# Issue order of weight splits and of the first matrix product in a one-core decoder kernel

## The chip, the cores and the metric

The kernel runs on one core of one Trainium2 chip. The metric is the device time of one execution in microseconds (us), as the median of several runs; lower is better. A core has five engines with queues of their own that are followed in order: TensorE (PE in the profile; its weight loads are PEld), VectorE (DVE), ScalarE (ACT), GpSimd (POOL) and SyncE (SP), which issues the DMA transfers here.

## The reference, cut to what matters

One step of a decoder layer, for a prompt of 2048 tokens and for 8 samples of 8 tokens that share all weights. The width is 1024, everything is float32.

```python
def _rmsnorm(x, g):
    x = x * lax.rsqrt(jnp.mean(x * x, axis=-1, keepdims=True) + 1e-5)
    return x * g

mem_k, mem_v = rmsnorm(mem, g_mem) @ w_ck, rmsnorm(mem, g_mem) @ w_cv   # 256 memory tokens
h = rmsnorm(x, g_mix)
q, k, v, u = split(h @ w_in)                     # 8 query heads, 2 kv heads, 512 pool channels
attn = window_attention(q, k, v, sinks)          # window 128, ALiBi
pool = pool_mixer(u) @ w_pool * pool_scale       # windows 2, 4, 8, 16
x = x + concat(attn, pool) @ w_out               # output projection
h = rmsnorm(x, g_cross)
p = softmax((h @ w_cq) @ mem_k.T / 16)           # 4 heads
x = x + (p @ mem_v) @ w_co                       # cross output
h = rmsnorm(x, g_ffn)
x = x + square(relu(h @ w_up)) @ w_down          # hidden 4096
y = rmsnorm(x, g_final)
```

The keys, values and pool histories are outputs too.

## The kernel before, in words

**Precision and splits.** Each float32 operand of a large product is split in two: a high part, rounded by a cast on ScalarE, and a low part, the difference, taken on VectorE. A product is then three matmuls per contraction step: high x high, high x low, low x high. For activations `rnd` (L94) and `Norm.apply` (L226) make the two parts. For weights the class `Stream` does it: `emit` (L125) takes the next item of one fixed list, loads its 512 KB through SP into one of six raw tiles `f` (L131), casts it into one `w` tile (L132) and subtracts into another (L133). There are twelve `w` tiles, so six weights can be split at once; a product gives a pair back when it has read it. `next` (L143) hands out a split weight and then calls `pump` (L137), which emits as long as two `w` tiles are free and fewer than five weights are ready.

**Order.** The program is written in one order, but the framework that builds the kernel decides the order of each engine's queue. It goes by readiness in a model of its own: of the instructions that are ready it takes the one that was written first, so a split that was written later can be queued ahead of an addition whose product isn't done yet. Waits between engines are put in by the framework. `tc.keep_in_program_order` (L214) holds the norm's matmul behind everything that was written before it on TensorE.

**Prologue** (L361). Fourteen warm-up matmuls of `ones` and `ident` (L366), whose result is not used; then the memory is loaded and split (L379, L380), its squares are summed (L202, L205, L206), and w_ck and w_cv are multiplied by it in sixteen chunks of 24 matmuls (`mm3`, L108: lines 111 to 113). After the third chunk the norm is finished (L404). Then w_cq and mem_k are folded into one matrix A, and mem_v and w_co into one matrix B. Both go through DRAM (`a_s`, `b_s`), stored by `put_fold` (L329).

**Superblocks** (L480). The tokens are worked in three superblocks of two blocks each, 384 and 384 tokens in the first two, 256 and 256 + 64 in the third. Each goes through:

- the input projection, attention and pooling, interleaved;
- the output projection: `dense` (L267) over eight chunks of 128 output columns for each block, 24 matmuls (L280 to L282) a chunk. Its `evac` is `add_evac` (L890): an addition to x on VectorE (L892), then `Norm.sq`, a Square on ScalarE (L205) and, for all but the first chunk, an addition to the sum of squares on GpSimd (L206). The last three chunks run for block 0 first and then for block 1;
- the norm of each block: `fin` (L209) is one matmul that sums over partitions (L214), two activations (L217, L218) and three operations on VectorE (L219 to L221); `apply` makes the normalised activations, eight steps of L232 on VectorE, L233 on ScalarE, and L235 on VectorE or GpSimd in turn. It is written one chunk after the block's last chunk, in pieces;
- the cross attention: `cross` (L912) takes the four weights of A's first half, then for each tile of 128 tokens 24 matmuls (lines 111 to 113), then A's second half. The fourth weight is read from the seventh contraction step on. In the third superblock the cross attention of the samples is interleaved (L966);
- the cross output: `dense` again, with B and `add_evac2` (L1091, addition L1093); its last four chunks run for block 0, then block 1;
- the feed-forward part, eight groups of `up` (L1138; evicted by L1130 to L1134) and `down` (L1143). The first group of `up` runs four chunks for block 0 and then four for block 1.

**Which splits stand around the ends.** When the eighth chunk of the output projection is fetched, three of its weights hold six `w` tiles, and the first three weights of A are emitted into the rest. After its last eviction is written, the next call of `next` emits three more: A's fourth weight and two of its second half. At the cross output four weights hold eight tiles, two weights of `up` are emitted ahead, and after the last eviction four more: the third and fourth chunk's of the first group and two of the second group.

Of the kernel before, what the change touches and what calls it, by code (L numbers as in the profile page):

```python
# [11 lines left out]
AF = mybir.ActivationFunctionType  # L12
ALU = mybir.AluOpType

P = 128
# [36 lines left out]
def kernel(ctx: ExitStack, tc: tile.TileContext, io, nW=12, nF=6, nT=8):  # L52
    nc = tc.nc
# [18 lines left out]
    ident = sb("ident", P)  # L72
    make_identity(nc, ident)
    ones = sb("ones", P)
# [16 lines left out]
    def f32(ap):  # L91
        return ap.bitcast(F32)
# [12 lines left out]
    def w8(t):  # L105
        return t[:].rearrange("p (k c) -> p k c", c=P)
# [8 lines left out]
    class Stream:  # L115
        def __init__(self):
            self.items = deque()
            self.ready = deque()
            self.resW = 0
            self.resF = 0  # L120

        def add(self, key, *raw, eng=None):
            self.items.append((key, raw, eng or nc.vector))

        def emit(self):  # L125
            key, raw, eng = self.items.popleft()
            th, tl = WS.get(), WS.get()
            r = FS.get()
            w = 1024 // len(raw)
            for i, src in enumerate(raw):  # L130
                nc.sync.dma_start(r[:, w * i:w * i + w], src)  # L131
            nc.scalar.copy(th[:], r[:, 0:1024])  # L132
            eng.tensor_tensor(tl[:], r[:, 0:1024], f32(th[:]), ALU.subtract)  # L133
            FS.put(r)
            self.ready.append((key, th, tl))

# [14 lines left out]
    S = Stream()  # L151
# [32 lines left out]
    class Norm:  # L184
# [4 lines left out]

        def sq(self, k, eng=None):  # L190
            n = self.n
            if self.on_pe:
                t = TS.get()
                if eng is None:
                    nc.scalar.activation(t[:, 0:n], self.x(k), AF.Square)
                else:
                    eng.tensor_tensor(t[:, 0:n], self.x(k), self.x(k), ALU.mult)
                nc.tensor.matmul(self.pm[:, 0:n], ones[:], t[:, 0:n], start=k == 0, stop=k == 7)
                TS.put(t)
            elif self.acc is None:  # L200
                self.acc = TS.get()
                nc.scalar.activation(self.acc[:, 0:n], self.x(k), AF.Square)  # L202
            else:
                t = TS.get()
                nc.scalar.activation(t[:, 0:n], self.x(k), AF.Square)  # L205
                self.add.tensor_tensor(self.acc[:, 0:n], self.acc[:, 0:n], t[:, 0:n], ALU.add)  # L206
                TS.put(t)

        def fin(self):  # L209
            n = self.n  # L210
# [56 lines left out]
    def dense(keys, blks, hi, lo, evac, head=2, tail=3, after=None, piece=8, seq=None):  # L267
        nch = len(keys)
        loaded, left, done = {}, {}, {0: 0, 1: 0}
        fetched = 0  # L270
        for c, b in seq or order(nch, head, tail):
            while fetched <= c:
                loaded[fetched] = S.next(keys[fetched])
                left[fetched] = 2
                fetched += 1
            th, tl = loaded[c]
            n = blks[b].n
            ps = MM.get()
            for k in range(8):
                nc.tensor.matmul(ps[:, 0:n], w8(th)[:, k, :], hi(b, k), start=k == 0, stop=False)  # L280
                nc.tensor.matmul(ps[:, 0:n], w8(th)[:, k, :], lo(b, k), start=False, stop=False)  # L281
                nc.tensor.matmul(ps[:, 0:n], w8(tl)[:, k, :], hi(b, k), start=False, stop=k == 7)  # L282
                if k < 7 and k % piece == piece - 1:
                    yield
            evac(c, b, ps)
            MM.put(ps)
            left[c] -= 1
            if left[c] == 0:
                WS.put(th, tl)
            flush()  # L290
            done[b] += 1
            if after is not None and done[b] == nch:
                later.append([DEF[b], lambda b=b: after(b)])
            yield
# [66 lines left out]
    def prologue():  # L361
        S.resW, S.resF = 1, 0
        mx = [XT[1][:, 0:1024], XT[1][:, 1024:2048]]
        mem = lambda k: mx[k // 4][:, 256 * (k % 4):256 * (k % 4 + 1)]
        warm = AUX.get()
        for _ in range(14):  # L366
            nc.tensor.matmul(warm[:, 0:P], ones[:], ident[:], start=True, stop=True)
        AUX.put(warm)
        nc.sync.dma_start(vec[:], io["vec"])
        nc.sync.dma_start(mx[0][:, 0:512], io["mem"][:, 0:512])  # L370
        S.emit()
        hm = Act(256)
        nm = Norm(256, mem, add=nc.vector)
        for i in range(4):
            if i:
                nc.sync.dma_start(mx[i // 2][:, 512 * (i % 2):512 * (i % 2) + 512], io["mem"][:, 512 * i:512 * (i + 1)])
            for k in range(2 * i, 2 * i + 2):
                g = vec[:, V_GMEM + k:V_GMEM + k + 1]
                nc.scalar.activation(hm.hi(k), mem(k), AF.Copy, scale=g)  # L379
                nc.vector.scalar_tensor_tensor(hm.lo(k), mem(k), g, f32(hm.hi(k)), ALU.mult, ALU.subtract)  # L380
        S.emit()
        for k in range(8):
            nm.sq(k)
        S.pump()
        def evac(a, dst, c, ps):
            t = TS.get()
            nc.vector.tensor_tensor(t[:, 0:256], ps[:, 0:256], nm.r[:, 0:256], ALU.mult)
            MM.put(ps)
            nc.sync.dma_start(dst[:, 256 * c:256 * (c + 1)], t[:, 0:256])
            rnd(t[:, 0:256], a.hi(c), a.lo(c))  # L390
            TS.put(t)

        pend, outs = [], []
        for name, dst in (("ck", io["mk"]), ("cv", io["mv"])):
            a = Act(256)
            outs.append(a)
            for c in range(8):
                th, tl = S.next((name, c))
                ps = MM.get()
                mm3(ps[:, 0:256], range(8), lambda k: w8(th)[:, k, :], lambda k: w8(tl)[:, k, :], hm.hi, hm.lo)  # L400
                WS.put(th, tl)
                pend.append((a, dst, c, ps))
                if name == "ck" and c == FINC:
                    nm.fin()  # L404
                if name == "cv" or c >= FINC:
                    while pend:
                        evac(*pend.pop(0))
                flush()
                if (name, c) == N1C:
                    norm1(blk[0][0], N1W)  # L410
        TS.put(nm.r)
        hm.free()
        mk, mv = outs
        norm1(blk[0][1], N1Q)
        for c in range(8):
            th, tl = S.next(("cq", c))
            for hf in range(2):
                ps = MM.get()
                for h2 in range(2):
                    ks = [(hf * 2 + h2) * 2, (hf * 2 + h2) * 2 + 1]  # L420
                    mm3(ps[:, 256 * h2:256 * h2 + 256], ks, lambda k: w8(th)[:, k, :], lambda k: w8(tl)[:, k, :], mk.hi, mk.lo)
                put_fold(ps[:], lambda o: [(a_s[hf, c // 2, :, 512 * (c % 2):512 * (c % 2) + 512], o[:, 0:512])])
                MM.put(ps)
            WS.put(th, tl)
            flush()
        mk.free()
        for h in range(4):
            w = [S.next(("co", 2 * h)), S.next(("co", 2 * h + 1))]
            for mb in range(2):
                for eh in range(2):  # L430
                    ps = MM.get()
                    mm3(ps[:], range(2),
                        lambda k: mv.hi(2 * h + k, mb * P, mb * P + P), lambda k: mv.lo(2 * h + k, mb * P, mb * P + P),
                        lambda k: w[k][0][:, 512 * eh:512 * eh + 512], lambda k: w[k][1][:, 512 * eh:512 * eh + 512])
                    kt = h * 2 + mb
                    put_fold(ps[:], lambda o: [(b_s[4 * eh:4 * eh + 4, :, P * kt:P * kt + P].rearrange("e p c -> p e c"),
                                                o[:, 0:512].rearrange("p (e c) -> p e c", c=P))])
                    MM.put(ps)
                flush()
            WS.put(*w[0], *w[1])  # L440
        mv.free()
# [38 lines left out]
    def superblock(s, blks, nxt):  # L480
        last = s == 2
# [3 lines left out]
        for kv in range(2):  # L485
            for hl in range(2):
                i = 2 * kv + hl
# [401 lines left out]

        def add_evac(c, b, ps):  # L890
            bl = blks[b]
            nc.vector.tensor_tensor(bl.x(c), ps[:, 0:bl.n], bl.x(c), ALU.add)  # L892
            bl.norm.sq(c)

        def mix_hi(hl):
            return lambda b, k: k4(blks[b].q[hl] if k < 4 else blks[b].d[hl], blks[b].n)[:, k % 4, :]
# [193 lines left out]

        def add_evac2(c, b, ps):  # L1091
            bl = blks[b]
            nc.vector.tensor_tensor(bl.x(c, 0, bl.np), ps[:, 0:bl.np], bl.x(c, 0, bl.np), ALU.add)  # L1093
            bl.norm.sq(c)

        def after_co(b):
            bl = blks[b]
# [240 lines left out]
```

## Time and profile before

| what | value |
|---|---|
| time, median of 3 runs | 2636.88 us (2635.72 to 2638.27) |
| profiled execution | span 2632.9 us; the median lies 4.0 us above it |
| VectorE busy | 1304.3 us (50%) |
| ScalarE busy | 982.1 us (37%) |
| GpSimd busy | 665.8 us (25%) |
| DMA | 244.76 MB, mean 93 GB/s |

The profile is one execution, taken by the hardware profiler. Busy time is the time in which an engine worked on an instruction; the ends of matmuls are modelled. A timeline row has start and duration in us, engine, line of the kernel, operation, output and inputs by their names, shape and count; the bracket at its end has the idle time of that engine before it and the event that ended it. A window row has the window, its length, and the busy time (and count) of PE, PEld, DVE, ACT and POOL, then the granted TensorE clock as a share, the busy share of the DMA engines, and GB/s. "SPq" rows are the issue of transfers.

### The profile page before, as it was taken

The page shows a single profiled execution, that of the slowest core. Times are in us where ns is not written, and L with a number is a line of the kernel's source. Part 1 is how long each engine was busy: PE and PEld are TensorE (multiplying, and loading weights), DVE is VectorE, ACT ScalarE, POOL GpSimd, SP SyncE. Part 2 cuts the span into 40 slices and gives each one's busy share as a digit, 9 for nine tenths or more (in the row PEclk, how much of TensorE's full clock was granted, in tenths as well). Part 3 has the DMA queues.
Part 4 walks back from the last instruction along what each step waited for, and adds up shares of the span by engine and source line. Part 5 has one row for each costly group of instructions (what it writes and reads, how often), then busy time and mean ns, then how long its engine had stood idle before and what let it go on. Part 6 is the DMA issues. An engine that isn't in the chain of part 4 may idle for free. (4 is left out here: it accounts for less than half of the span.)

```text
span 2632.9 us, 39258 instructions
## 1 busy us (share of the span) xinstructions
PE 2565.7 (97%) x15753; PEld 2461.6 (93%) x15753; DVE 1304.3 (50%) x2283; ACT 982.1 (37%) x1923; POOL 665.8 (25%) x723
## 2 busy tenths in 40 slices
PE   8899999999999999999999999999999999999998
PEld 8799989999999999997999999999999669999998
DVE  7567453533333367936363333334766646344334
ACT  6666342422222244824342222223354434322231
POOL 2215322311111153433241111113324214111111
PEclk9999999999999999999999999999999999999999
DMA  7843211211111123131111111112414473222210
GB/s 276 257 130 104 71 47 64 73 65 64 65 65 64 56 70 108 55 123 57 65 63 60 63 64 64 65 57 70 141 60 146 178 269 117 81 81 83 87 57 37
DMA packets 92539, 244.76 MB, mean 93 GB/s; under 512 B 16772, under 2 KB 31556, under 8 KB 91204
## 3 DMA queue, kind: packets, MB, share of 16 engines
q1 hardware_dynamic: 92356, 242.25, 27.0%
q8 instruction: 123, 2.02, 0.3%
q14 instruction: 60, 0.49, 0.1%
HBM read 219.53 MB, written 22.69 MB: 92 GB/s over the span
## 5 line engine op out<-in xcount | busy, mean ns | idle before, releaser
L280 PE MATMUL mm<-act,w 128*128 128x384 f32 (+2 forms) x2784 | 903.0, 324 | 2.6 <-ACT act L631 1.6
L281 PE MATMUL mm<-act,w 128*128 128x384 f32 (+2 forms) x2784 | 897.7, 322 | 0.7 <-DVE act L632 0.5
L282 PE MATMUL mm<-act,w 128*128 128x384 f32 (+2 forms) x2784 | 897.1, 322 | 1.2 <-DVE w L133 1.2
L132 ACT CAST w<-f 128x1024 fp32r<-128x1024 f32 x330 | 346.0, 1050 | 734.7 <-PE mm L112 459.7
L133 DVE TENSOR_TENSOR w<-f,w 128x1024 fp32r<-128x1024 f32 x330 | 425.3, 1294 | 304.7 <-ACT w L132 304.5
L111 PE MATMUL mm<-act,w 128*128 128x384 f32 (+2 forms) x1728 | 552.4, 320 | 9.3 <-ACT w L132 7.6
L113 PE MATMUL mm<-act,w 128*128 128x384 f32 (+2 forms) x1728 | 549.2, 318 | 0.5 <-DVE w L133 0.5
L112 PE MATMUL mm<-act,w 128*128 128x384 f32 (+2 forms) x1728 | 548.9, 318 | 0.0
L280 PEld LDWEIGHTS mm<-act,w 128*128 128x128 f32 x2784 | 527.6, 189 | 7.4 <-issue 2.6
L281 PEld LDWEIGHTS mm<-act,w 128*128 128x128 f32 x2784 | 527.3, 189 | 7.3 <-issue 2.6
L282 PEld LDWEIGHTS mm<-act,w 128*128 128x128 f32 x2784 | 527.2, 189 | 2.0 <-DVE w L133 1.7
L1131 POOL TENSOR_TENSOR t<-t 128x384 f32<-128x384 f32 (+2 forms) x192 | 216.2, 1126 | 1039.5 <-ACT t L1130 1039.5
L1164 DVE TENSOR_TENSOR x<-mm,x 128x384 f32<-128x384 f32 (+2 forms) x384 | 199.8, 523 | 327.9 <-PE mm L113 327.9
L111 PEld LDWEIGHTS mm<-act,w 128*128 128x128 f32 x1728 | 327.2, 189 | 11.3 <-ACT w L132 7.6
L112 PEld LDWEIGHTS mm<-act,w 128*128 128x128 f32 x1728 | 327.1, 189 | 1.0
L113 PEld LDWEIGHTS mm<-act,w 128*128 128x128 f32 x1728 | 327.0, 189 | 0.8 <-DVE w L133 0.8
L206 POOL TENSOR_TENSOR t<-t,t 128x384 f32<-128x384 f32 (+2 forms) x161 | 191.4, 1190 | 344.7 <-ACT t L205 311.7
L1134 DVE TENSOR_TENSOR act<-t,act 128x384 fp32r<-128x384 f32 (+2 forms) x192 | 102.9, 536 | 305.4 <-ACT act L1133 305.4
L1133 ACT CAST act<-t 128x384 fp32r<-128x384 f32 (+2 forms) x192 | 93.4, 487 | 235.3 <-POOL t L1131 235.3
L205 ACT ACTIVATE t<-x 128x384 f32<-128x384 f32 (+2 forms) x140 | 68.3, 498 | 153.1 <-DVE x L1093 75.6
L1130 ACT ACTIVATE t<-mm 128x384 f32<-128x384 f32 (+2 forms) x192 | 88.3, 460 | 93.2 <-PE mm L282 91.9
L111 PE MATMUL mm<-w,act 128*128 128x512 f32 x288 | 117.1, 409 | 3.0 <-ACT w L132 2.7
(187 smaller groups left out, 2211.8 us busy)
## 6 DMA issues: line engine op xcount, KB each, us to landing
f<-in_wup SPq DMA_DIRECT2D x96, 512.0 KB, 3.5
f<-in_wdn SPq DMA_DIRECT2D x96, 512.0 KB, 3.5
f<-in_win SPq DMA_DIRECT2D x30, 512.0 KB, 3.7
f<-a_s SPq DMA_DIRECT2D x24, 512.0 KB, 3.3
f<-b_s SPq DMA_DIRECT2D x24, 512.0 KB, 4.2
x<-in_x SPq DMA_DIRECT2D x6, 1536.0 KB, 7.0
f<-in_wco SPq DMA_DIRECT2D x16, 512.0 KB, 5.5
f<-in_cmk SPq DMA_DIRECT2D x16, 512.0 KB, 4.5
```

What stands on the lines that cost most here:

```text
L111: nc.tensor.matmul(ps, Wh(k), Hh(k), start=first and i == 0, stop=False)
L112: nc.tensor.matmul(ps, Wh(k), Hl(k), start=False, stop=False)
L113: nc.tensor.matmul(ps, Wl(k), Hh(k), start=False, stop=final and i == last)
L132: nc.scalar.copy(th[:], r[:, 0:1024])
L133: eng.tensor_tensor(tl[:], r[:, 0:1024], f32(th[:]), ALU.subtract)
L206: self.add.tensor_tensor(self.acc[:, 0:n], self.acc[:, 0:n], t[:, 0:n], ALU.add)
L280: nc.tensor.matmul(ps[:, 0:n], w8(th)[:, k, :], hi(b, k), start=k == 0, stop=False)
L281: nc.tensor.matmul(ps[:, 0:n], w8(th)[:, k, :], lo(b, k), start=False, stop=False)
L282: nc.tensor.matmul(ps[:, 0:n], w8(tl)[:, k, :], hi(b, k), start=False, stop=k == 7)
L1131: nc.gpsimd.tensor_tensor(q[:, 0:n], r[:, 0:n], r[:, 0:n], ALU.mult)
L1134: nc.vector.tensor_tensor(lo, q[:, 0:n], f32(hi), ALU.subtract)
L1164: nc.vector.tensor_tensor(bl.x(m), ps[:, 0:n], bl.x(m), ALU.add)
```

## The change

Three ties are added with `tc.issue_after(i)`: what the block under it writes for the engine of instruction `i` is queued behind `i` on that engine. It sets the order of that queue only, and adds no wait for `i` to finish; no operation, transfer or tile is added or removed.

- `dense` keeps what its last `evac` returned in `S.behind`. `add_evac` and `add_evac2` return their addition (VectorE) and their Square (ScalarE) for the last chunk of block 1, and nothing else does. So the weights emitted between that eviction and the next `dense`'s first eviction have their cast queued behind that Square, and their subtraction behind that addition. The loads of the raw weights are outside the block and not tied.
- The first product of the prologue (w_ck, chunk 0) is queued behind the last warm-up matmul on TensorE.

```diff
@@ class Stream
+            self.behind = []
...
-            nc.scalar.copy(th[:], r[:, 0:1024])
-            eng.tensor_tensor(tl[:], r[:, 0:1024], f32(th[:]), ALU.subtract)
+            with ExitStack() as held:
+                for i in self.behind:
+                    held.enter_context(tc.issue_after(i))
+                nc.scalar.copy(th[:], r[:, 0:1024])
+                eng.tensor_tensor(tl[:], r[:, 0:1024], f32(th[:]), ALU.subtract)
@@ Norm.sq
-                nc.scalar.activation(t[:, 0:n], self.x(k), AF.Square)
+                i = nc.scalar.activation(t[:, 0:n], self.x(k), AF.Square)
...
+            return i
@@ dense
-            evac(c, b, ps)
+            last = evac(c, b, ps)
+            S.behind = last or []
@@ prologue
-            nc.tensor.matmul(warm[:, 0:P], ones[:], ident[:], start=True, stop=True)
+            wu = nc.tensor.matmul(warm[:, 0:P], ones[:], ident[:], start=True, stop=True)
...
-                mm3(ps[:, 0:256], range(8), lambda k: w8(th)[:, k, :], lambda k: w8(tl)[:, k, :], hm.hi, hm.lo)
+                if name == "ck" and c == 0:
+                    with tc.issue_after(wu.ins):
+                        mm3(ps[:, 0:256], range(8), lambda k: w8(th)[:, k, :], lambda k: w8(tl)[:, k, :], hm.hi, hm.lo)
+                else:
+                    mm3(ps[:, 0:256], range(8), lambda k: w8(th)[:, k, :], lambda k: w8(tl)[:, k, :], hm.hi, hm.lo)
@@ add_evac (add_evac2 likewise, with the prompt's columns)
-            nc.vector.tensor_tensor(bl.x(c), ps[:, 0:bl.n], bl.x(c), ALU.add)
-            bl.norm.sq(c)
+            i = nc.vector.tensor_tensor(bl.x(c), ps[:, 0:bl.n], bl.x(c), ALU.add)
+            j = bl.norm.sq(c)
+            return [i.ins, j.ins] if (c, b) == (7, 1) else None
```

More of the change, by code (lines that the diff above doesn't have):

```diff
@@ L1092, in add_evac2 @@
             bl = blks[b]
-            nc.vector.tensor_tensor(bl.x(c, 0, bl.np), ps[:, 0:bl.np], bl.x(c, 0, bl.np), ALU.add)
-            bl.norm.sq(c)
+            i = nc.vector.tensor_tensor(bl.x(c, 0, bl.np), ps[:, 0:bl.np], bl.x(c, 0, bl.np), ALU.add)
+            j = bl.norm.sq(c)
+            return [i.ins, j.ins] if (c, b) == (7, 1) else None
         def after_co(b):
```

1 line of the change is left out of this document (added).

## The prediction

> **What bounds the kernel now.** I read the page's span and busy rows first, then TensorE's own list of waits (engine, tile and line, the releaser; total us, times, longest).
>
> ```profile
> span 2632.9 us, 39258 instructions
> PE 2565.7 (97%) x15753; PEld 2461.6 (93%) x15753; DVE 1304.3 (50%) x2283; ACT 982.1 (37%) x1923; POOL 665.8 (25%) x723
> ...
> PE aux L214 <- POOL t L206: 20.7, 9, 3.7
> ```
>
> TensorE is busy 97% of the span, so only time in which it stands still, or works at the wrong moment, can be won: 67.2 us in all. The largest single wait is the norm's one matmul (L214), which waits for the sum of squares (L206) nine times, 20.7 us together. Six of the nine stand where this change acts, once after each output projection and once after each cross output. Next I read the timelines of the start and of these places (start, duration, engine, line; in brackets the idle time before it and its releaser).
>
> ```profile
> 7.57 0.58 PE L111 MATMUL mm<-act,w 128*128 128x256 f32 x1 [7.57 <-ACT w L132]
> ...
> 9.21 0.42 PE L111 MATMUL mm<-act,w 128*128 128x256 f32 x1
> ...
> 9.43 0.41 PE L112 MATMUL mm<-act,w 128*128 128x256 f32 x1
> ...
> 9.64 5.62 PE L367 MATMUL aux<-ident,ones 128*128 128x128 f32 x28
> ...
> 15.02 0.36 PE L113 MATMUL mm<-act,w 128*128 128x256 f32 x1
> ...
> 23.02 0.28 PE L113 MATMUL mm<-act,w 128*128 128x256 f32 x1
> ...
> 8.69 2.46 DVE L380 SCALAR_TENSOR_TENSOR act<-x,vec,act 128x256 fp32r<-128x256 f32 x6
> ...
> 11.93 1.22 DVE L133 TENSOR_TENSOR w<-f,w 128x1024 fp32r<-128x1024 f32 x1
> ...
> 13.93 1.22 DVE L133 TENSOR_TENSOR w<-f,w 128x1024 fp32r<-128x1024 f32 x1
> ...
> 1.01 0.29 POOL masks.py:199 TENSOR_SCALAR_AFFINE_SELECT ident<-ident 128x128 f32<-128x128 f32 x1
> ```
>
> At the start TensorE waits 7.57 us for the first weight, does five products, and only then runs the warm-up (L367, 14 matmuls shown as 28), 5.62 us in which real work is ready. Its input, ident, was finished at 1.30.
>
> **First product behind the warm-up.** From 1.30 the 5.62 us of warm-up end at about 7.0, inside the wait that exists anyway; its cost becomes zero, and if it overran it would cost the overrun alone. What is late next? The first chunk needs the low halves of the memory activations: L380 ends at 8.69 + 2.46 = 11.15. The second chunk needs its weight's low half at 11.93 + 1.22 = 13.15, from where 22 products are left. Between 15.02 and 23.02 lie 67 products, 0.119 us each; so the second chunk ends issuing at 15.8. The third has its low half at 15.15 and ends at 15.8 + 24 x 0.119 = 18.6. Before, that was 23.02: 4.4 us gained. Against it: at 9.21 to 9.43 two products stand 0.22 apart. If the 19 products left in chunk one behind 9.43 still ran at that pace, it would end at 13.6, chunk two (a third of it slow) at about 17.2 and chunk three at 20.0: 3.0 gained. I take 4.0, nearer the first, since the warm-up then stands before the products.
>
> [...]
>
> Everything behind the third chunk (norm, evictions, stores and loads on SP) follows in order and moves with it. What could hold it back is the stage of the folds, where DMA is nearly full:
>
> ```profile
> 100.00:120.00 20.00, 17.24 (x68) 13.39 (x67) 5.24 (x5) 11.18 (x18) 1.17 (x1) 0.91 0.95 292
> ```
>
> (The last three columns are clock, DMA share and GB/s.) I keep the 4.0, since these transfers too are issued by steps that move.
>
> **Splits behind the output projection.** By the slots, three pairs of weights are split after the seventh chunk's eviction in the program: the fourth weight of A's first half, and two of its second. The cast of the first was taken early:
>
> ```profile
> 308.86 1.05 ACT L132 CAST w<-f 128x1024 fp32r<-128x1024 f32 x1 [2.81 <-PE mm L281]
> ...
> 322.52 0.55 DVE L892 TENSOR_TENSOR x<-mm,x 128x384 f32<-128x384 f32 x1
> ...
> 323.15 0.52 ACT L205 ACTIVATE t<-x 128x384 f32<-128x384 f32 x1
> ...
> 324.35 1.97 POOL L206 TENSOR_TENSOR t<-t,t 128x384 f32<-128x384 f32 x1
> ...
> 322.56 0.39 PE L111 MATMUL mm<-w,act 128*128 128x512 f32 x1
> 322.79 0.40 PE L112 MATMUL mm<-w,act 128*128 128x512 f32 x1
> ...
> 326.38 0.91 PE L214 MATMUL aux<-t,ones 128*128 128x384 f32 x2 [1.44 <-POOL t L206]
> ...
> 2060.79 0.45 PE L111 MATMUL aux<-act,act 128*64 128x512 f32 x1 [2.28 <-ACT act L233]
> ```
>
> The last addition (L892, 322.52) stays: it is queued behind the other block's norm on VectorE, not behind splits. But the first cross tile needs that fourth weight at its seventh contraction step, 322.56 (high) and 322.79 (low). Tied behind the Square, the cast runs 323.67 to 324.7 and the subtraction to 325.9, or 326.7 if it collides with L206 (0.77, worked out below); I take 326.3. So the product stalls at 322.56 to 324.7 and again to 326.3; five more products at 0.23 us end at 327.5, where L214 goes at once, its 1.44 wait gone (L206, 1.22 to 1.97 long, ends at 325.6 to 326.3). 327.5 against 326.38: **1.1 us lost**, 0.7 to 1.5 by the collision. If products of the next tile were placed into the stall, it would be a gain of up to 1.4. The second group repeats it. In the third the L214 is as late, but a wait of 2.28 us for the next norm follows (2060.79); it takes up part, and I put 0.8. Together **+3.0** (-4 to +5).
>
> **Splits behind the cross output.** Here four pairs are tied.
>
> ```profile
> 463.86 4.00 DVE L133 TENSOR_TENSOR w<-f,w 128x1024 fp32r<-128x1024 f32 x2
> 467.78 0.55 DVE L1093 TENSOR_TENSOR x<-mm,x 128x384 f32<-128x384 f32 x1
> ...
> 472.80 0.55 DVE L219 SCALAR_TENSOR_TENSOR t<-t 128x384 f32<-128x384 f32 x1
> ...
> 468.42 0.52 ACT L205 ACTIVATE t<-x 128x384 f32<-128x384 f32 x1 [3.39 <-DVE x L1093]
> ...
> 12.61 3.88 ACT L132 CAST w<-f 128x1024 fp32r<-128x1024 f32 x4
> ...
> 469.09 1.22 POOL L206 TENSOR_TENSOR t<-t,t 128x384 f32<-128x384 f32 x1 [2.31 <-ACT t L205]
> ...
> 485.48 1.02 POOL L235 TENSOR_TENSOR act<-t,act 128x384 fp32r<-128x384 f32 x1 [1.04 <-ACT act L233]
> ...
> 470.36 0.91 PE L214 MATMUL aux<-t,ones 128*128 128x384 f32 x2 [3.69 <-POOL t L206]
> ...
> 487.43 0.33 PE L281 MATMUL mm<-act,w 128*128 128x384 f32 x1
> ```
>
> The addition (L1093) does stand behind two splits: it moves from 467.78 to 463.86. The Square ended 1.16 behind it (468.42 + 0.52), so now at 465.0, and L206 2.53 behind it, so at 466.4, or 467.2 with a collision. TensorE came to L214 at 470.36 - 3.69 = 466.67, so the wait goes. But what is late next is the same norm's other end. L217's input is there, yet ScalarE first does four casts (3.88 us, to 468.9) and VectorE four subtractions: from 466.05, 4 x 1.22 gives 470.9, and 0.77 more for each that meets a POOL add (two took 4.00, not 2.46), up to 472.4. L219 then stands at 471.4 to 473.0; I take 472.4, 0.4 earlier than 472.80. The second block's first product needs the last of this norm: L235 ends at 486.50, its reader is at 487.43, so 0.93 us is all the slack. TensorE, some 3.5 us earlier, waits there. Gain: 0.4 + 0.93 = **1.3**, not 3.7 (0.7 to 2.3).
>
> [...]
>
> ```profile
> 1345.80:1349.10 3.30, 2.91 (x7) 2.31 (x8) 0.21 (x1) 1.23 (x3) 1.12 (x2) 0.50 0.70 231
> 470.40:473.80 3.40, 3.40 (x18) 3.13 (x19) 1.44 (x3) 1.41 (x3) 0.69 (x1) 1.00 0.58 186
> ...
> 1346.19 1.65 PE L214 MATMUL aux<-t,ones 128*128 128x384 f32 x2 [3.66 <-POOL t L206]
> ...
> 1349.36 0.55 DVE L219 SCALAR_TENSOR_TENSOR t<-t 128x384 f32<-128x384 f32 x1
> ...
> 1364.63 0.33 PE L281 MATMUL mm<-act,w 128*128 128x384 f32 x1
> ...
> 2203.47 1.76 DVE L133 TENSOR_TENSOR w<-f,w 128x1024 fp32r<-128x1024 f32 x1
> ...
> 2210.15 0.49 DVE L219 SCALAR_TENSOR_TENSOR t<-t 128x320 f32<-128x320 f32 x1
> ...
> 2221.02 0.90 POOL L235 TENSOR_TENSOR act<-t,act 128x320 fp32r<-128x320 f32 x1 [0.92 <-ACT act L233]
> ...
> 2221.98 0.41 PE L281 MATMUL mm<-act,w 128*128 128x320 f32 x1
> ```
>
> In the second group the same wait was followed by 3.3 us at a granted clock of 0.50 (1.65 us lost); in the first it was not. Its wait began at 1342.53, 875.86 behind the first group's, so its L219 would stand at 472.4 + 875.86 = 1348.3, 1.1 earlier; L235 ends 13.70 behind L219 as in the first group, at 1363.06, its reader is at 1364.63, a slack of 1.6: gain **2.7**. In the third there is no slack (2221.92 to 2221.98). The addition can go at 2203.47, its Square ends 1.16 later, a cast of 1.05 follows, and four subtractions end at 2210.6, or 2211.3 with a clash; behind them L219 comes 0.9 **later** than 2210.15 (0 to 1.9). Together **-3.1** (-12, when all three waits and two slow stretches are won, to +1).
>
> The moved splits issue no transfer of their own, but free the raw tiles later, so loads on SP go some 15 us later (as the cast moves from 308.86 to 323.67); what they load is six splits ahead, so I cost it at nothing, and at the length of one split, 1.22, if that lead were gone.
>
> **Sum.** -4.0 + 3.0 - 3.1 = -4.1. The profiled span of 2632.9 becomes 2628.8; the median lies 4.0 above the span (2636.88), so 2632.8. This is 0.16%; about 0.2% (5.3 us) is what a measurement of this kernel can tell from no change.
>
> **Rivals.** *Waits really go.* If the norm's steps get ahead of the casts behind the cross output, its three waits come back: 3 x 3.2 (3.69 less the half us that is left) and one slow stretch of 1.65, so -4.0 + 3.0 - 11.3 = -12.3, 2624.6; if the cross tile doesn't stall either, six waits by the mean of 20.7 / 9 = 2.3 and two slow stretches, -21, 2616. For it: L214's wait is the largest of TensorE's. Against: slack of 0 to 1.6 behind it.
> *The start's gain is lost in the folds.* DMA at 0.95 sets its own pace, and -4.0 becomes 0: -0.1, 2636.8. Against: the transfers are issued in order behind steps that move.
> *Slower: the late fourth weight.* Each stall of 3.6 us under the output projection is followed by a slow stretch: 3 x (1.1 + 1.65) = 8.3, with the start's gain down to 1 and nothing from the cross output, +7.3, 2644.2. It decides if the clock falls in all three groups and the start gives under 3. Against: it needs both.
>
> **How the numbers follow.** My forecast 0.48 (own range 2629 to 2638; a fifth of it beyond the 0.2%), waits go 0.31, folds 0.11, late weight 0.10. Faster: 0.31 + 0.10 = 0.41. Slower: most of the last, 0.09. Within: 0.50. The range leaves out the far end of the first rival and most of the slower one: 2623 to 2640.
>
> **What would show it.** Right: the warm-up before the first product, and the third chunk ended near 19; L111 of the first cross tile waiting for the cast L132 about 2 us; L214 with next to no wait; waits of 1 to 3 us for L233 or L235 in the second block's first up chunk. Wrong: L1093 still behind splits; the folds ending no earlier; L219 over 2 us earlier.

## The result, and the profile after

The changed kernel takes 2627.82 us (median of 16 runs, 2623.66 to 2634.12), the kernel before 2635.23 us on the same chip (16 runs, 2630.37 to 2639.82): a ratio of 0.9974, with a 95% interval of 0.9966 to 0.9982. The medians lie 7.4 us apart. The forecast was 2632.8 us, 4.1 us less; the time lies inside its range, but beyond the 0.2% that it had called the likeliest (the near end of the interval is 0.18%).

Lines move by a few in the new code: the cast L132 is now L136, the split's subtraction L133 is L137, Square L205 is L210, the squares' addition L206 is L211, the norm's matmul L214 is L220, L219 is L225, the apply's L233 and L235 are L239 and L241, the dense products L280 to L282 are L286 to L288, the additions L892 and L1093 are L903 and L1105, the warm-up L367 is L374.

The first rows of the profile's page and TensorE's list of waits, in the changed kernel:

```profile
span 2622.0 us, 39268 instructions
PE 2562.3 (98%) x15753; PEld 2457.1 (94%) x15753; DVE 1300.5 (50%) x2283; ACT 982.8 (37%) x1923; POOL 657.9 (25%) x723
```

```profile
PE mm L111 <- ACT w L136: 9.9, 7, 3.0
PE aux L220 <- POOL t L211: 7.9, 4, 2.7
...
PE mm L287 <- POOL act L241: 1.5, 3, 0.5
```

TensorE stands still for 59.7 us instead of 67.2. The norm's matmul waits 4 times for 7.9 us instead of 9 times for 20.7; of these four, 1.42 us is behind the third cross output, and the other three stand where the change does not act. Part of what was won is now spent on a split weight (L111 for L136: 2.40, 2.41 and 2.34 of the 9.9 us stand in the first cross tile of each superblock), and a little on the first block's apply (L287 for L241). L111 had 10.3 us before too, but there 7.6 of it was the wait for the very first weight:

```profile
PE mm L111 <- ACT w L132: 10.3, 3, 7.6
```

The timeline of the start. The warm-up runs in the idle time, the first chunk's products then follow 0.11 us behind one another (9.12, 9.23), and the next matmul behind the third chunk's last, the L220 of the memory's norm, starts at 18.89. The first row below is of the kernel before, where that matmul started at 23.14.

```profile
23.14 0.60 PE L214 MATMUL aux<-t,ones 128*128 128x256 f32 x2
```

```profile
1.35 6.06 PE L374 MATMUL aux<-ident,ones 128*128 128x128 f32 x28 [1.35 <-POOL ident masks.py:199]
7.63 0.38 PE L111 MATMUL mm<-act,w 128*128 128x256 f32 x1 [0.22 <-ACT w L136]
...
9.12 0.28 PE L111 MATMUL mm<-act,w 128*128 128x256 f32 x1
9.23 0.28 PE L112 MATMUL mm<-act,w 128*128 128x256 f32 x1
...
18.89 0.60 PE L220 MATMUL aux<-t,ones 128*128 128x256 f32 x2
```

The timeline where the first output projection ends (the column behind the two times names the engine):

```profile
317.74 0.51 PE L113 MATMUL mm<-w,act 128*128 128x512 f32 x1
320.64 0.92 PE L111 MATMUL mm<-w,act 128*128 128x512 f32 x2 [2.40 <-ACT w L136]
321.36 0.63 PE L112 MATMUL mm<-w,act 128*128 128x512 f32 x1
...
324.34 0.85 PE L220 MATMUL aux<-t,ones 128*128 128x384 f32 x2
...
318.49 0.55 DVE L903 TENSOR_TENSOR x<-mm,x 128x384 f32<-128x384 f32 x1
320.62 3.52 DVE L137 TENSOR_TENSOR w<-f,w 128x1024 fp32r<-128x1024 f32 x3 [1.58 <-ACT w L136]
...
319.79 0.99 POOL L211 TENSOR_TENSOR t<-t,t 128x384 f32<-128x384 f32 x1
```

L220 has lost its wait of 1.44, and L211 takes 0.99 instead of 1.97, since the subtractions start only when it is nearly done (320.62, where it ends at 320.78); before, two ran beside it, and took 3.95 for both where three take 3.52 here:

```profile
323.45 3.95 DVE L133 TENSOR_TENSOR w<-f,w 128x1024 fp32r<-128x1024 f32 x2
```

In exchange the seventh contraction step (L111) stands 2.40 us for the cast of A's fourth weight, and the products behind it run at 0.63 each instead of 0.40.

The timeline where the first cross output ends:

```profile
459.87 1.01 DVE L1105 TENSOR_TENSOR x<-mm,x 128x384 f32<-128x384 f32 x2
462.48 5.93 DVE L137 TENSOR_TENSOR w<-f,w 128x1024 fp32r<-128x1024 f32 x4 [1.59 <-ACT w L136]
468.33 0.55 DVE L1147 TENSOR_TENSOR act<-t,act 128x384 fp32r<-128x384 f32 x1
468.80 0.55 DVE L225 SCALAR_TENSOR_TENSOR t<-t 128x384 f32<-128x384 f32 x1
...
461.40 3.88 ACT L136 CAST w<-f 128x1024 fp32r<-128x1024 f32 x4
...
480.57 1.18 POOL L241 TENSOR_TENSOR act<-t,act 128x384 fp32r<-128x384 f32 x1 [1.04 <-ACT act L239]
...
463.39 0.86 PE L220 MATMUL aux<-t,ones 128*128 128x384 f32 x2
...
481.80 0.44 PE L287 MATMUL mm<-act,w 128*128 128x384 f32 x1 [0.53 <-POOL act L241]
```

The addition stands ahead of all four splits, and L220 starts with no wait (before: 3.69). The four splits now stand between the addition and L225, and the other end of the norm is what TensorE meets: L287 waits 0.53 for the last L241.

**Where the time went.** TensorE does the same 15,753 matmuls in both kernels. I number them in order of start and take, for the same number, the start in a run's profile less the start in the profile of before. The table has how much this difference moves over the start (to 70 us) and over each of the six places (marks, on the clock of before: 317 to 339, 1180 to 1219, 2045 to 2082 for the output projections; 462 to 492, 1338 to 1368, 2198 to 2225 for the cross outputs). Negative is earlier. The mark at 339 lies just ahead of a wait for the softmax's result (L919 in the kernel before), which gives back another 0.3 in the rows where the two weights of A's second half are held back: behind it the change stands at +1.0, and the versions with A's fourth weight free at -1.1.

| us | start | output proj. 1 | 2 | 3 | cross output 1 | 2 | 3 |
|---|---|---|---|---|---|---|---|
| forecast | -4.0 | +1.1 | +1.1 | +0.8 | -1.3 | -2.7 | +0.9 |
| the change | -3.7 | +1.3 | +0.6 | -0.1 | -2.4 | -3.7 | +0.9 |
| the change again | -3.6 | +1.2 | -0.4 | +0.2 | -2.4 | -3.7 | +0.4 |
| start's tie alone | -3.9 | 0.0 | -0.1 | +0.5 | +1.6 | +0.2 | +0.9 |
| output projection's tie alone | -0.4 | +1.2 | -0.4 | 0.0 | +1.5 | +0.2 | 0.0 |
| cross output's tie alone | -1.5 | 0.0 | 0.0 | +0.5 | -2.4 | -3.8 | 0.0 |
| start and cross output | -3.9 | 0.0 | -0.1 | +0.8 | -2.4 | -3.8 | +0.6 |
| output projection's, A's fourth weight free | +0.4 | -0.8 | -1.3 | -0.6 | +2.4 | +1.2 | 0.0 |
| cross output's on VectorE alone | -0.4 | 0.0 | -0.1 | +0.7 | -2.1 | -3.5 | +0.7 |
| two splits held back to the norm's end | -2.2 | -0.8 | -1.3 | +1.3 | -1.0 | -2.4 | +2.9 |
| the change, A's fourth weight free | -2.1 | -0.8 | -1.3 | +0.8 | -2.4 | -3.7 | -0.1 |

The change's own row sums to -7.1, next to the 7.4 of the medians. Its profile ends 11.0 earlier; about 3 of the rest are two stretches at half clock that the profile of before has, and this one has not at those places. Its windows (the third column from the end is the granted clock):

```profile
1888.50:1891.80 3.30, 3.30 (x18) 3.30 (x17) 2.44 (x5) 1.46 (x3) 0.00 (x0) 0.50 0.54 41
1929.50:1932.80 3.30, 3.30 (x15) 2.82 (x14) 1.53 (x4) 1.39 (x4) 0.00 (x0) 0.50 0.50 165
```

Such stretches, each about 3.4 us long (some twice that) and worth half of that, 1.7 (an estimate from the clock of 0.50), recur at a few places in every profile, near 1930 for one; many others lie elsewhere in each. The start differs by up to 1.5 even without its tie. So a single profile's end says little here, and each step must be read at its own place.

### The profile page after: what moved, and what is told of

It reads as the page before. It is cut to its first block, busy times and chain, and to the rows that moved or that the text cites. A ratio compares the mean times of both kernels' runs of the same rounds, so it can differ in the third digit from the quotient of the medians.

```text
span 2622.0 us, 39268 instructions
## 1 busy us (share of the span) xinstructions
PE 2562.3 (98%) x15753; PEld 2457.1 (94%) x15753; DVE 1300.5 (50%) x2283; ACT 982.8 (37%) x1923; POOL 657.9 (25%) x723
## 5 line engine op out<-in xcount | busy, mean ns | idle before, releaser
L286 PE MATMUL mm<-act,w 128*128 128x384 f32 (+2 forms) x2784 | 901.1, 324 | 2.8 <-ACT act L642 1.6
L287 PE MATMUL mm<-act,w 128*128 128x384 f32 (+2 forms) x2784 | 897.0, 322 | 3.4 <-POOL act L241 1.5
L288 PE MATMUL mm<-act,w 128*128 128x384 f32 (+2 forms) x2784 | 895.6, 322 | 1.4 <-DVE w L137 1.4
L136 ACT CAST w<-f 128x1024 fp32r<-128x1024 f32 x330 | 344.3, 1049 | 702.7 <-PE mm L112 457.6
L137 DVE TENSOR_TENSOR w<-f,w 128x1024 fp32r<-128x1024 f32 x330 | 418.4, 1276 | 305.7 <-ACT w L136 304.8
L111 PE MATMUL mm<-act,w 128*128 128x384 f32 (+2 forms) x1728 | 552.3, 320 | 2.8 <-DVE t L394 2.2
L287 PEld LDWEIGHTS mm<-act,w 128*128 128x128 f32 x2784 | 525.7, 189 | 12.7 <-POOL act L241 3.7
L286 PEld LDWEIGHTS mm<-act,w 128*128 128x128 f32 x2784 | 525.8, 189 | 7.6 <-issue 2.3
L288 PEld LDWEIGHTS mm<-act,w 128*128 128x128 f32 x2784 | 525.6, 189 | 2.2 <-DVE w L137 2.0
L1144 POOL TENSOR_TENSOR t<-t 128x384 f32<-128x384 f32 (+2 forms) x192 | 216.4, 1127 | 1038.6 <-ACT t L1143 1038.6
L1177 DVE TENSOR_TENSOR x<-mm,x 128x384 f32<-128x384 f32 (+2 forms) x384 | 199.7, 523 | 327.5 <-PE mm L113 327.5
L111 PEld LDWEIGHTS mm<-act,w 128*128 128x128 f32 x1728 | 326.8, 189 | 4.7 <-ACT t L207 2.4
L211 POOL TENSOR_TENSOR t<-t,t 128x384 f32<-128x384 f32 (+2 forms) x161 | 182.2, 1132 | 337.0 <-ACT t L210 329.6
L210 ACT ACTIVATE t<-x 128x384 f32<-128x384 f32 (+2 forms) x140 | 68.0, 498 | 161.7 <-DVE x L1105 74.5
L111 PE MATMUL mm<-w,act 128*128 128x512 f32 x288 | 116.5, 407 | 9.7 <-ACT w L136 9.7
```

Source lines behind the costliest of these rows:

```text
L111: nc.tensor.matmul(ps, Wh(k), Hh(k), start=first and i == 0, stop=False)
L1144: nc.gpsimd.tensor_tensor(q[:, 0:n], r[:, 0:n], r[:, 0:n], ALU.mult)
L1177: nc.vector.tensor_tensor(bl.x(m), ps[:, 0:n], bl.x(m), ALU.add)
```

## The experiments

My theory after the result: the start's gain is kept through the folds; the tie behind the output projection loses about 3 us and the tie behind the cross output wins more than I had put, because the norm's other end had more room than I had worked out. The rivals: that the start's gain is lost in the folds and the cross output has all of it, or that all three waits behind the cross output come back in full.

### One part at a time

The start's tie alone (both evictions return nothing to be tied behind):

```diff
-            return [i.ins, j.ins] if (c, b) == (7, 1) else None
+            return None
```

> Only the first product is tied behind the warm-up; both ties of the weight splits are left out. Theory (three parts that add up): the warm-up moves into the wait for the first weight, the third chunk ends near 18.7 us instead of 23.0, and 3.7 us are still won at 70 us and at the end of the span, apart from half-clock stretches that fall where they fall (1.7 us each). Waits of the norm's matmul under the output projection and the cross output stay as before: 1.4, 1.4, 1.0 and 3.7, 3.7, 3.1 us. Time 0.9986 of before. Rival (the folds swallow it): the gain is gone by 125 us, ratio 1.000. Rival (all of the change's gain is the start): ratio 0.997, as the whole change.

Measured: 2633.9 us, ratio 0.9991 (0.9982 to 1.0). The steps: -3.9 at 70 us, and between -2.5 and -4.7 all the way through the folds and the first superblock. The start's gain is kept; in the time it is 2.4 us, and its interval reaches from none to 4.7, so the time alone would not have settled it.

The output projection's tie alone (the first product isn't tied, and `add_evac2` returns nothing):

```diff
-                if name == "ck" and c == 0:
+                if False:
```

> Only the splits behind the output projection are tied. Theory: a loss. The first cross tile waits for the cast of A's fourth weight, 2.4 us in the first two superblocks, the norm's wait of 1.4 us goes, net 1.0 us lost in each of the first two, and between 0.3 won and 0.8 lost in the third: 1.7 to 3 us slower, ratio 1.0007 to 1.001. Rival (the tie does what its place suggests): the waits of 1.4, 1.4 and 1.0 us go and nothing takes their place, 3.8 us faster, ratio 0.9985.

Measured: 2637.47 us, ratio 1.0005 (0.9995 to 1.0015): no gain, and a loss of up to 4 us is within the interval. In the steps the first group loses 1.2, but the second wins 0.4 and the third is even: the loss that was expected in each is there in one.

The cross output's tie alone (as above, and `add_evac` returns nothing instead):

> Only the splits behind the cross output are tied. Theory: the norm's waits of 3.7, 3.7 and 3.1 us shrink to nearly 0, 0 and 1.4, and short waits for the same norm's activations come in the second block's first chunk; net 2.7 us won in the first superblock, 2.7 to 3.8 in the second (by the half clock), 0.8 lost in the third: 4.6 to 5.7 us faster, ratio 0.998. Rival (all of the change's gain is the start): ratio 1.000. Rival (the waits go and nothing follows): 10.4 us and more, ratio 0.996.

Measured: 2627.23 us, ratio 0.9964 (0.9951 to 0.9977). This one tie has the whole of the change's gain and perhaps more.

The start and the cross output without the output projection's tie:

> The change without its tie behind the output projection: warm-up tie and cross-output tie. Theory: -3.7 and -4.6 to -5.7 add, 8.3 to 9.4 us faster than before, 1.7 to 3 us faster than the whole change, ratio 0.9966. Rival (the tie behind the output projection is worth something): slower than the whole change, ratio above 0.9974.

Measured: 2625.12 us, ratio 0.9959 (0.9945 to 0.9973). Beside the change's 0.9974 this would make the output projection's tie cost about 4 us; the intervals overlap, so it is the steps that carry this: 0.0 in the first group against +1.2 or +1.3 with the tie.

### Which splits, and which engine

The output projection's tie alone, with A's fourth weight left where the framework puts it; only the two weights of A's second half are held back:

```diff
-                for i in self.behind:
+                for i in self.behind if key[0] != "A" or key[2] == 1 else []:
```

> As the tie behind the output projection alone, but the fourth weight of A's first half is left free; only the two weights of the second half are tied. Theory (the loss is the cast of that one weight, late for the first cross tile): the wait of 2.4 us for it goes in the first two superblocks, and since no split runs beside the last sum of squares, that sum takes 1.0 instead of 2.0 us and the norm's wait falls from 1.4 to about 0.4: 1.0 us won a group instead of 1.0 lost, 2 to 3 us faster than before, ratio 0.999. Rival (the loss comes from the other splits, queued ahead of the norm): the wait for the cast is only moved to another weight, ratio 1.0005 as with all three tied.

Measured: 2634.03 us, ratio 0.9992 (0.9983 to 1.0001). The first group now gains 0.8 where the full tie lost 1.2, and the second gains 1.3 where it gained 0.4. The late fourth weight is what the tie costs; holding back the other two pays. In the second group, where neither profile has a stretch at half clock, that weight costs 0.9; in the first it is 2.0, and there the full tie has such a stretch.

The cross output's tie on the subtractions alone (the casts are free; the other two ties are left out as before):

```diff
-            return [i.ins, j.ins] if (c, b) == (7, 1) else None
+            return [i.ins] if (c, b) == (7, 1) else None
```

> Only the subtractions of the four splits are tied behind the addition of the cross output; their casts are free again. Theory (the addition is held up by subtractions on VectorE, and the casts cost the other block's norm on ScalarE): the addition still moves ahead, but the first block's norm runs up to 0.8 us later than with both tied; the second block's norm starts earlier on ScalarE, and still has the four subtractions ahead of it on VectorE. First two superblocks within 1 us of the 2.6 and 3.3 won with both tied; third at 0 to 1 won instead of 0. Ratio 0.997 to 0.998. Rival (the casts ahead of the norm are what the third superblock loses): 3 us won there.

Measured: 2626.78 us, ratio 0.9966 (0.9952 to 0.9979), and steps of -2.1, -3.5 and +0.7. Its timeline has L220 waiting for longer:

```profile
466.10 0.91 PE L220 MATMUL aux<-t,ones 128*128 128x384 f32 x2 [1.57 <-POOL t L211]
```

So 1.57 us of the norm's wait may stay with hardly any change to the sum: L220 starts later, and TensorE has that much less to wait at the norm's other end. The gain comes from the addition standing ahead of the subtractions, and it ends where the apply ends. The third group's 0.7 lost speaks against the rival: free casts win nothing there.

### An attempt at the other end

Since four splits between the addition and L225 hold the norm's end, this kernel emits only two of them there, tied as before; the other two are emitted later and tied behind the second block's norm. A's fourth weight is free:

```diff
+            self.cap = 5
...
-            while self.items and len(WS.free) - 2 >= self.resW and len(self.ready) < 5:
+            while self.items and len(WS.free) - 2 >= self.resW and len(self.ready) < self.cap:
...
-            bl.norm.fin()
+            ends = bl.norm.fin()
+            if b == 1:
+                S.behind, S.cap = ends, 5
...
+        S.cap = 3
```

(`fin` returns its Exp and its last VectorE operation.)

> The change with A's fourth weight free, and behind the cross output only two splits tied as before; the two of the second group are put behind the second block's norm. Theory: 3.7 from the start, 2 from the output projections, and behind the cross outputs 3.5, 4 and 2.5 won, as the norm no longer waits for two casts and two subtractions: 13 to 16 us faster than before, ratio 0.9945. Rival (the slack behind the norm is used up, and what is late next is the product's own operands): as warm-up and cross-output tie alone, 9 us, ratio 0.996.

Measured: 2628.88 us, ratio 0.9972 (0.9963 to 0.9981). The theory failed: the cross outputs give -1.0, -2.4 and +2.9, worse than the change's in all three groups. Its timeline shows why:

```profile
467.74 0.55 DVE L226 SCALAR_TENSOR_TENSOR t<-t 128x384 f32<-128x384 f32 x1
...
469.39 1.22 DVE L138 TENSOR_TENSOR w<-f,w 128x1024 fp32r<-128x1024 f32 x1
...
474.16 1.21 DVE L138 TENSOR_TENSOR w<-f,w 128x1024 fp32r<-128x1024 f32 x1
...
483.14 1.17 POOL L243 TENSOR_TENSOR act<-t,act 128x384 fp32r<-128x384 f32 x1 [1.04 <-ACT act L241]
...
484.36 0.45 PE L289 MATMUL mm<-act,w 128*128 128x384 f32 x1 [0.54 <-POOL act L243]
```

(L226, L138, L243 and L289 are this kernel's numbers for the change's L225, L137, L241 and L287.) L225's counterpart does start earlier: at 467.74, which is 469.67 on the clock of before (the place is entered 1.93 earlier), against the change's 468.80 + 3.13 = 471.93. But the two subtractions that were held back now run inside the apply, which takes 483.14 + 1.17 - 467.74 = 16.6 us instead of 480.57 + 1.18 - 468.80 = 12.95. The two subtractions take 2.4 of the 3.6 by which it is longer; their two casts on ScalarE (1.99 us, from 467.15) and what else shifted weren't tried apart. Work taken out of one end of the norm came back in the other.

### The warm-up, and the best version

The start and cross output kernel with one warm-up matmul in place of fourteen; thirteen whose result isn't used are left out:

```diff
-        for _ in range(14):
+        for _ in range(1):
```

> Warm-up tie and cross-output tie, but with one warm-up matmul instead of fourteen (their result isn't used). Theory (the warm-up releases the clock before the first product): the first chunk's products then stand 0.22 us apart instead of 0.12, the third chunk ends at 20.0 to 20.5 instead of 18.7 us, so 1.3 to 1.8 us are lost at the start. Rival (it does nothing for the products): the third chunk ends at 18.7.

Measured: one run of 2627.98 us, which says nothing by itself. At the start L220 comes 0.65 later than in the change (19.54 against 18.89), and 0.9 later than in the kernel that it was made from (18.68):

```profile
1.36 0.80 PE L374 MATMUL aux<-ident,ones 128*128 128x128 f32 x2 [1.36 <-POOL ident masks.py:199]
...
9.19 0.41 PE L112 MATMUL mm<-act,w 128*128 128x256 f32 x1
9.41 0.41 PE L113 MATMUL mm<-act,w 128*128 128x256 f32 x1
...
19.54 0.60 PE L220 MATMUL aux<-t,ones 128*128 128x256 f32 x2
```

The products stand 0.22 apart, as they did before the change, instead of 0.11 with the warm-up ahead. The loss is less than expected, since the chunks also wait for their weights' low halves. So of the start's 4.25 us (18.89 against 23.14) most comes from the warm-up no longer standing between the products, and about a microsecond from the pace. Two things qualify this. The warm-up does not make sure of the pace: in a second profile of the change ("the change again", the last experiment below) it ran ahead too, yet the granted clock was 0.50 from 9.3 to 12.7, and most of the first chunk's products stood 0.21 apart. And that slow first chunk cost nothing: L220 came 11.25 behind the first product, against 11.26 in the change, as the second chunk waits for its weight's low half anyway. With one warm-up matmul it came 12.20 behind; there the slow pace reaches into the second chunk. That the warm-up releases the clock, as the theory had it, is not shown: with one warm-up matmul no clock record stands ahead of 14.2, and the distance of the products is all that was measured.

The whole change with A's fourth weight free, and the change once more on the same chip:

> The whole change, with A's fourth weight left free (nothing put behind the second block's norm). Theory: what the parts gave in their own runs adds up: 3.9 at the start, 0.9 and 1.2 at the first two output projections, 2.6 and 3.3 at the first two cross outputs, nothing in the third superblock: 11.9 us faster than before, ratio 0.9955, and 3.5 to 4 us faster than the whole change in the same call. Rival (the two output-projection gains are taken back by the norm that follows): as warm-up and cross-output tie alone, ratio 0.9966.

> The change as it stands, timed on the same chip beside the kernel with A's fourth weight free. Theory: ratio 0.9971 (-3.9 at the start, +1.0 and +1.1 at the output projections, -2.6 and -3.3 at the cross outputs: 7.7 us faster), and 3.5 to 4 us slower than that kernel; the stretches at half clock lie in other places than in its first profile. Rival (the steps shown are in that one profile alone): other steps at the same places.

Measured: 2625.57 us (five runs, 2620.33 to 2625.87), ratio 0.9956 (0.9944 to 0.9969), and for the change again 2628.15 us (2624.54 to 2630.18), ratio 0.9969 (0.9957 to 0.9981). The version with the fourth weight free beats the kernel before; against the change its median is 2.6 us lower, and the intervals still overlap. The rival, 0.9966, lies within its interval, and beside the start and cross output kernel (0.9959) no gain is shown in the time; that the fourth weight is best left free rests on the steps. In the change again, the start, the first output projection and the first two cross outputs come back within 0.1 of the first profile; the second output projection comes at -0.4 in place of +0.6, without the slow stretch, and the third cross output at +0.4 in place of +0.9. In the timeline of the version with the fourth weight free, the cross tile runs through its seventh step, and L220 waits 0.56:

```profile
317.45 0.39 PE L112 MATMUL mm<-w,act 128*128 128x512 f32 x1
...
318.95 0.50 PE L113 MATMUL mm<-w,act 128*128 128x512 f32 x1 [0.43 <-DVE act L241]
...
322.94 0.91 PE L220 MATMUL aux<-t,ones 128*128 128x384 f32 x2 [0.56 <-POOL t L211]
```

## Why the prediction was right or wrong

**The start: right.** The forecast was -4.0 between 3.0 and 4.4; the third chunk ends 4.25 us earlier, and 3.6 to 3.9 us are left at 70 us in four of the six profiles that have the tie and all the warm-up. In the other two, at -2.1 and -2.2, a stretch at half clock near 25 us goes with it (half of 3.4, 1.7). That the products behind the warm-up run at the pace of the later ones (0.119 us), which set the 4.0 nearer the 4.4, was an estimate: they stood 0.11 apart in the change, and 0.21 in its second profile. The rival of the folds fell: the gain passes through them in the start's tie alone.

**Behind the output projection: the size about right, the working not.** I put a stall for the cast until 324.7, then a second one for the low half, and L214 at 327.5, 1.1 late. The stall came: L111 starts at 320.64, which is 324.8 on the clock of before (the stage is entered 4.14 earlier). The second stall all but vanished (0.09 at most in these profiles): three products of the next tile stand ahead of L220 that did not before, and fill the time until the low half is there, what I had named as a possible gain. Where the clock stays at full, as in the output projection's tie alone in its second group, L220 comes 0.9 late, but has 0.7 us of the next tile's work (three products of 0.23) ahead of it, so the tie costs about 0.2 there. The rest is the clock, the mechanism of the slower rival. Of the six profiled places with the full tie (first and second groups of the change, the change again and the tie alone), four have a stretch at 0.50 behind the stall of 2.40. Three of them, in the first group, lose 1.2 to 1.3, and the change's second group 0.6; the two without it win 0.4:

```profile
325.00:328.40 3.40, 3.00 (x7) 2.43 (x8) 3.02 (x3) 2.24 (x3) 0.55 (x1) 0.50 0.22 48
1203.50:1206.90 3.40, 3.22 (x12) 2.21 (x13) 3.33 (x3) 1.94 (x3) 0.24 (x1) 1.00 0.27 88
```

These are two windows of the output projection's tie alone, behind the same wait of 2.4 in the first and in the second group; the last three columns are clock, DMA share and GB/s. In the third group the tied profiles are 1.0 to 1.3 late at 2069.6, but by 2082 they lie with or ahead of the untied ones; the predicted +0.8 is not seen.

**Behind the cross output: the mechanism right, the term too small.** This is the step that was furthest off: -1.3, -2.7 and +0.9 were put, -2.4, -3.7 and +0.9 (+0.4, 0.0 and -0.1 in other runs) measured. What was late next is what I said, the apply's last L241 with a slack of 0.93 behind it, and that slack is used up (a wait of 0.53 at 481.80, where I had put 1 to 3). But the way there was shorter twice over. L225 starts at 468.80, which is 471.93 on the clock of before (the place is entered 3.13 earlier), 0.87 ahead of 472.80 where I took 0.4: both additions run back to back from 459.87, and the four subtractions, two of them beside additions on GpSimd (L211 and L1144), took 5.93 where I allowed up to 6.4. And the apply behind it takes 12.95 us instead of 13.70, while I had kept it as it was. Why it is shorter was not tried: neither kernel has a split inside it, and the evictions of `up` that run between its steps fall at other points. So 0.87 + 0.75 + 0.93 less 0.05 makes 2.5, next to the 2.4 seen. The third group, where no slack was found, came as worked out.

**The clock behind the waits: not counted enough.** I read from one profile that the wait of 3.69 was followed by a slow stretch in the second group and not in the first, and took that as the state of the first. In the other profiles that still have this wait (start's tie alone, output projection's tie alone, and with the fourth weight free) every first and second group has one:

```profile
466.90:470.30 3.40, 3.40 (x13) 3.40 (x12) 2.41 (x5) 1.28 (x3) 0.00 (x0) 0.50 0.37 142
1344.20:1347.50 3.30, 3.30 (x12) 3.30 (x11) 2.04 (x4) 1.41 (x3) 0.00 (x0) 0.50 0.55 174
```

(The start's tie alone, both groups.) That is 7 of 8 places with the wait, and none of 14 in the seven profiles in which L220 starts there without a wait. In the first group the profile of before is thus the lucky case (the last section shows how its wait lay): against a usual run the gain there is, by estimate, 2.4 + 1.7 = 4.1. That may be why the cross output's tie alone shows 9.5 us in the median (2635.32 x 0.0036; 6.1 to 12.9) where its steps at the cross outputs sum to 6.2 against this one profile; the interval holds both.

**The sum.** -4.1 was put; the steps gave -7.1 and the medians -7.4. By the time alone, -7.4 lies between this forecast and the rival in which the waits really go, at -12.3, so it is the rows that decide between them: two of the three L214 waits did go, as the rival says, but L225 is 0.87 earlier and not the 3.2 that it needs. Part of its price, the slow stretch, was real; its 3 x 3.2 was too high by itself, as the third wait was 3.1 and not 3.69.

## What to carry to other kernels

When a wait goes, cost what the waiting work meets next, both the start and the length of each step on the way, since moving work out of a stretch can shorten steps that ran beside it (here the last sum of squares, 0.99 us instead of 1.97). Before holding work back as a group, ask for each member when it is first read: here one weight of three was due within the stall and cost what the other two won. And where the same wait is followed by a drop of TensorE's clock in some profiles only (here 2.40 us in 4 of 6 places, 3.69 in 7 of 8), compare several profiles of the same place, for one of them may be the lucky one.

## What the runs showed of the hardware

**Equal waits, and a clock that fell behind some of them.** In the first two groups a wait of TensorE of 0.56 was followed by a stretch at 0.50 in none of 6 places, 1.43 in 2 of 12, 2.40 in 4 of 6, and 3.69 in 7 of 8. What differs between equal waits shows against the clock records of the twelve profiles: within a profile, all changes of the granted clock lie whole multiples of 3.413 us apart, to 0.004 us. I lay a grid of this step over TensorE's rows, through these changes, and count its windows from 20 us on, taking those at full clock. Where TensorE stood idle for 1.9 us or more within a window, the next was at 0.50 in 58 of 58 cases; with 1.1 to 1.9 us idle in 27 of 128; with less in 12 of 8,847, and these are one place in each profile, near 1930, where TensorE works on small products (L801 in the kernel before, 128x32 each, from 1933.75). (Idle time goes by the modelled ends of matmuls.) Two grid windows of the kernel before and two of the start's tie alone, in the first group:

```profile
465.10:468.51 3.41, 1.57 (x10) 1.25 (x8) 3.41 (x4) 0.09 (x1) 1.68 (x1) 1.00 0.40 141
468.51:471.92 3.41, 1.56 (x7) 1.29 (x8) 0.95 (x1) 1.42 (x4) 2.01 (x2) 1.00 0.76 228
463.49:466.91 3.42, 1.09 (x4) 0.82 (x5) 1.43 (x2) 1.04 (x3) 2.01 (x2) 1.00 0.93 261
466.91:470.32 3.41, 3.41 (x12) 3.41 (x12) 2.43 (x5) 1.27 (x3) 0.00 (x0) 0.50 0.34 139
```

In the kernel before, the wait of 3.69 is cut into 1.84 and 1.85 us of idle time by the border at 468.51, and the clock stays; in the other, 2.33 us of it fall into one window, and the next is at half clock. Apart from the 12 near 1930, no window with under 1.1 us idle was followed by half clock in these profiles. That it is the idle time of a window which drops the clock is my reading of these counts; no run tried it alone.

**The clock column can miss a slow start.** Two windows from 7.6 to 10.6, of the change and of the kernel with one warm-up matmul, in this order:

```profile
7.60:10.60 3.00, 2.21 (x16) 2.01 (x17) 2.99 (x6) 3.00 (x9) 0.00 (x0) 1.00 1.03 416
```

```profile
7.60:10.60 3.00, 2.54 (x11) 2.24 (x12) 3.00 (x7) 2.61 (x8) 0.00 (x0) 1.00 1.03 412
```

Both say 1.00, yet 11 products take more busy time (2.54 us) than 16 (2.21). The second profile has no clock record ahead of 14.2, and the column reads 1.00 where there is none; the first one's records start at 7.0. At the start the pace has to be read from the distance of the rows.
